# Later turns for the bias pieces, the right-hand sums and the first head loads; norm weights in the output weights; another root in the last step

## The chip, the cores and the metric

The kernel runs on one core of one Trainium2 chip. The metric is the device time of one execution in microseconds (us): the median of the runs. Before the change it is 1885.63 us (three runs, 1884.32 to 1886.45). Engines: PE is TensorE, DVE is VectorE, ACT is ScalarE, POOL is GpSimd, SP is SyncE, which here only issues DMAs.

## The reference

One encoder layer on x of 1024 tokens by 1024 features, float32. `rmsnorm(x, g)` is `x * rsqrt(mean(x*x) + 1e-6) * g`, `swiglu` is `(silu(x @ w_gate) * (x @ w_up)) @ w_down` with an inner width of 2816.

```python
h = swiglu(rmsnorm(x, ffn1_pre_g), ffn1_w_gate, ffn1_w_up, ffn1_w_down)
x = x + 0.5 * rmsnorm(h, ffn1_post_g)
q, k, v = heads(rmsnorm(x, mix_pre_g) @ w_qkv)        # 16 heads of 64
o_na  = neighbourhood_attention(q[:8], k[:8], v[:8], na_rel_bias)
o_dil = dilated_mixture_attention(q[8:], k[8:], v[8:], t5_rel_bias)
mixed = concat(rmsnorm(o_na, na_out_g), rmsnorm(o_dil, dil_out_g)) @ w_out
x = x + rmsnorm(mixed, mix_post_g)
h = swiglu(rmsnorm(x, ffn2_pre_g), ffn2_w_gate, ffn2_w_up, ffn2_w_down)
return x + 0.5 * rmsnorm(h, ffn2_post_g)
```

## The kernel before

Every float32 product is made of three matmuls: each operand is split into a rounded high part (ACT, a cast: `whi`, `hi`) and the rest (DVE, a subtraction: `wlo`, `lo`), and L268 to L270 multiply high by high, high by low and low by high. The large products also use a 2 by 2 block scheme with seven products in place of eight; its sums of weight blocks and of token blocks are made on DVE, and its partial results are combined on DVE and ACT as they leave PSUM. The names of the blocks are A11, A12, A22, S1 to S4 on the token side, T1 and T2 on the weight side.

The stages in order of time: the first norm and the first product rows (to about 80 us); the first feed-forward network, FFN1, with 22 blocks of gate and up weights (to about 460 us; a block in its full form takes about 19.3 us, the early ones 13.6 us), then the passes of its down product (`Passes`, tiles `pw`, `praw`); values and then q and k (`QKPairs`, about 700 to 910 us, the last of them 8 turns of 19.3 us); the dilated and the neighbourhood attention (about 910 to 1150 us); the output projection; the second feed-forward network (called FFN3 here, as in the code, about 1210 to 1882 us), whose last pass gives the output.

What sets the order of the work: PE's program is written by hand. Beside it stand queues that are drained as PE's program is written. `c.sums` and `c.steps` hold small closures, one of each run at every second slice of four of a product (`step`); `c.todo` holds one list of closures per block, a *turn* (`tick`, `plan`); `flush` runs all that is left at once. `one_a_turn` puts one step of a list into each turn from `first` on. `behind(f, engines)` ties what f records behind the last instruction recorded so far on these engines; without it a list scheduler of the language layer places the instruction on its engine by its own estimates. A queue of DMAs is in order of its engine: a DMA that waits on SP or POOL holds up those behind it.

The pieces that the change touches. *Right-hand sums* (`RightSums`, L314 to L337): for each of 11 pairs of down-weight blocks, two loads `tr` by SP (L324, L325, 1 MB), three subtractions in place on DVE (L333 to L335), and a store `ts<-tr` to DRAM by POOL (L336); the load of the next pair goes into the same single buffer, so it waits for the store to land. *Bias pieces* (`bias_steps`): tables made once, stores `nb`, `gab` and `stk` by POOL, spread over the turns of FFN1. *Head loads* (`load_head`): for a head of attention, `st<-qk` by POOL (L920, L921), `g<-gab`, and with a pair's first head `va` and `vb`, by SP (L983, L971, L975); `queued` runs it behind the turn's other work. *Operand* (`norm`, `tile`, `sums`, `put`): the norm of the tokens, its block sums (L240) and its transposes on PE (L176) with their two evictions (L177 on ACT, L178 on DVE). *Finish* (L723 on): square sums on ACT (L168), the gain (L730), the inverse root (L137 to L154), the residual (L747 or L762). *GroupNorm*: the norm of an attention group, L1234 for the scale, L1246 to L1251 for the transposes (`put`). *Weights* (L116, L117): the output weights, split in high and low.

At the end of a feed-forward network's blocks, `final` closes the memory of the weight loads and opens `praw`, the buffers of the down product's loads (L635, L638), in the same memory.

## Time and profile before

| | |
|---|---|
| median of the runs | 1885.63 us (1884.32 to 1886.45) |
| the profiled execution | 1884.22 us |
| its span, first to last instruction | 1882.5 us |
| busy: PE, DVE, ACT, POOL | 1840.9, 1318.3, 789.3, 324.2 us |
| mean granted TensorE clock | 0.995 |
| end of the last matmul, issue of the last output DMA | 1871.78, 1879.22 us |

The profiled execution is 1.72 us longer than its span; the times of the profile's rows count from the span's start. A row of the timeline gives start and duration in us, engine, line, operation, output and input tiles, and in brackets the idle time before it and what ended that. A row of the windows gives, for a stretch of the span, the busy time of each engine with its count of instructions, then the granted clock, the busy share of the DMA engines and what they moved. Busy times of PE count each matmul of 128 by 512 with 0.39 us, though the next starts 0.23 us later, so a PE that seems always busy is read better by its count of matmuls per stretch.

### The profile page before, as it was taken

The numbers are of one execution on the slowest core, as the hardware profiler recorded it, in microseconds if no ns is written. First come the engines' busy times: TensorE is split into PE (matmuls) and PEld (weight loads), VectorE is DVE, ScalarE is ACT, GpSimd is POOL, SyncE is SP. The second block draws the span as 40 slices with busy tenths as digits, with TensorE's granted clock in tenths as the row PEclk, the third lists the DMA queues.
The fourth block names the chain that finished last, engine by engine and source line by source line (L and its number), as shares of the span: only waits on it lengthen the run. The fifth ranks groups of instructions, "written<-read, shape, count | busy, mean of one in ns | idle before, by whom it ended". The sixth has DMA issues, their size and how long they took to land.

```text
span 1882.5 us, 25100 instructions
## 1 busy us (share of the span) xinstructions
PE 1840.9 (98%) x9048; PEld 1536.6 (82%) x9048; DVE 1318.3 (70%) x2212; ACT 789.3 (42%) x1283; POOL 324.2 (17%) x521
## 2 busy tenths in 40 slices
PE   7999999999999999999899999999999999999997
PEld 6878878888888878888799987878888788888886
DVE  7778787766565876577666766786878877654557
ACT  5422233334443546223477764453222333344342
POOL 2122122111000122222442300121111111110000
PEclk9999999999999999999999999999999999999999
DMA  7656676755986666658783732585456656486563
GB/s 273 222 195 208 188 266 227 242 186 201 345 290 205 246 211 225 210 178 263 236 283 113 253 129 79 178 306 176 157 190 223 241 203 233 178 296 205 190 225 134
DMA packets 164222, 405.15 MB, mean 215 GB/s; under 512 B 17857, under 2 KB 34465, under 8 KB 162050
## 3 DMA queue, kind: packets, MB, share of 16 engines
q1 hardware_dynamic: 114896, 228.82, 36.8%
q0 software_dynamic: 48336, 172.63, 25.7%
q10 hardware_dynamic: 866, 2.10, 0.3%
q8 instruction: 71, 1.16, 0.3%
q14 instruction: 53, 0.43, 0.1%
HBM read 277.47 MB, written 131.07 MB: 217 GB/s over the span
## 4 chain that ended last, share of the span: by engine, by line
PE 56%; issue 27%; DMA 7%; DVE 6%; POOL 3%; ACT 2%; SPq 0%; POOLq 0%; DVEq 0%; ACTq 0%
PE mmp L268 9%; PE mmp L270 9%; PE mmp L269 9%; PE accp L270 6%; PE accp L268 6%; PE accp L269 6%; PE po L1068 3%; DMA tr<-in_wd_dram 2%; PE ptp L956 2%; PE sp L1056 1%; DMA ts<-tr 1%; PE trp L176 1%; PE po L1189 1%; POOL g L591 1%; PE sp L1176 1%
## 5 line engine op out<-in xcount | busy, mean ns | idle before, releaser
L268 PE MATMUL mmp<-x,whi 128*128 128x512 f32 x1412 | 558.8, 396 | 10.0 <-DVE v L499 7.3
L270 PE MATMUL mmp<-x,wlo 128*128 128x512 f32 x1412 | 553.3, 392 | 3.0 <-DVE wlo L363 3.0
L269 PE MATMUL mmp<-x,whi 128*128 128x512 f32 x1412 | 552.6, 391 | 0.2 <-DVE x L1527 0.2
L268 PEld LDWEIGHTS mmp<-x,whi 128*128 128x128 f32 x1412 | 265.6, 188 | 70.6 <-issue 6.2
L270 PEld LDWEIGHTS mmp<-x,wlo 128*128 128x128 f32 x1412 | 265.5, 188 | 63.3 <-DVE wlo L363 4.4
L269 PEld LDWEIGHTS mmp<-x,whi 128*128 128x128 f32 x1412 | 265.8, 188 | 56.2 <-DVE x L1527 0.5
L640 DVE TENSOR_TENSOR pw<-praw,pw 128x1024 fp32r<-128x1024 f32 (+1 forms) x182 | 199.0, 1139 | 124.4 <-ACT pw L639 124.4
L362 ACT CAST whi<-wraw 128x1024 fp32r<-128x1024 f32 x126 | 132.0, 1050 | 330.8 <-PE mmp L269 258.0
L639 ACT CAST pw<-praw 128x1024 fp32r<-128x1024 f32 (+1 forms) x182 | 168.9, 983 | 203.6 <-PE accp L270 170.0
L268 PE MATMUL accp<-pw 128*128 128x512 f32 x600 | 234.4, 391 | 0.2 <-DVE hb L711 0.2
L270 PE MATMUL accp<-pw 128*128 128x512 f32 x600 | 233.5, 389 | 0.0
L269 PE MATMUL accp<-pw 128*128 128x512 f32 x600 | 233.4, 389 | 0.0
L363 DVE TENSOR_TENSOR wlo<-wraw,whi 128x1024 fp32r<-128x1024 f32 x126 | 153.8, 1223 | 19.9 <-ACT whi L362 19.9
L268 PEld LDWEIGHTS accp<-pw 128*128 128x128 f32 x600 | 112.6, 188 | 23.9 <-issue 0.6
L270 PEld LDWEIGHTS accp<-pw 128*128 128x128 f32 x600 | 112.6, 188 | 23.6
L269 PEld LDWEIGHTS accp<-pw 128*128 128x128 f32 x600 | 112.7, 188 | 23.0
L572 POOL DMA_DIRECT2D g<-sg x44 | 24.1, 548 | 424.7 <-DVE sg L565 253.4
L381 ACT COPY s<-mmp 128x512 f32<-128x512 f32 x52 | 30.5, 587 | 125.1 <-PE mmp L270 112.6
L528 DVE TENSOR_TENSOR c<-mmp,u 128x512 f32<-128x512 f32 x52 | 35.8, 688 | 53.6 <-PE mmp L270 53.6
L178 DVE TENSOR_TENSOR x<-trp,x 128x512 fp32r<-128x512 f32 x76 | 52.0, 688 | 24.9 <-ACT x L177 24.7
L453 DVE TENSOR_TENSOR wraw<-wraw 128x1024 f32<-128x1024 f32 x52 | 63.5, 1220 | 6.1 <-DMA wraw<-in_wqk_dram 5.4
L177 ACT CAST x<-trp 128x512 fp32r<-128x512 f32 x76 | 44.5, 587 | 42.6 <-PE trp L176 42.4
(281 smaller groups left out, 2788.6 us busy)
## 6 DMA issues: line engine op xcount, KB each, us to landing
praw<-g SPq DMA_DIRECT2D x70, 512.0 KB
wraw<-in_wg_dram SPq DMA_DIRECT2D x44, 512.0 KB
wraw<-in_wu_dram SPq DMA_DIRECT2D x44, 512.0 KB
tr<-in_wd_dram SPq DMA_DIRECT2D x44, 512.0 KB
g<-sg POOLq DMA_DIRECT2D x88, 256.0 KB, 4.3
ts<-tr POOLq DMA_DIRECT2D x22, 1024.0 KB, 5.0
praw<-ts SPq DMA_DIRECT2D x88, 256.0 KB
praw<-in_wd_dram SPq DMA_DIRECT2D x66, 256.0 KB
```

The source lines that it names most:

```text
L177: nc.scalar.copy(hi, ps)
L178: nc.vector.tensor_sub(lo, ps, hi.bitcast(F32))
L268: nc.tensor.matmul(out, ahi, bhi, start=start, stop=False, skip_group_check=go_on)
L269: nc.tensor.matmul(out, ahi, blo, start=False, stop=False, skip_group_check=go_on)
L270: nc.tensor.matmul(out, alo, bhi, start=False, stop=stop, skip_group_check=go_on)
L362: nc.scalar.copy(hi, raw)
L363: nc.vector.tensor_sub(lo, raw, hi.bitcast(F32))
L453: nc.vector.tensor_sub(r[:, 0:2], r[:, 1:3], r[:, 0:2])
L639: nc.scalar.copy(w[side][:, 0, :m], raw[:, :m])
L640: nc.vector.tensor_sub(w[side][:, 1, :m], raw[:, :m], w[side][:, 0, :m].bitcast(F32))
L956: c.nc.tensor.transpose(self.tps[:, j, :], self.probs[:, j * P:(j + 1) * P], c.ident)
L1068: nc.tensor.matmul(po[0][:, un * 2 + j], u.pt[:, 2 * j + t, :], rhs, start=t == 0, stop=t == 1)
```

## The change

In words, part by part:

1. *Output weights.* The gains `na_out_g` and `dil_out_g` are no longer multiplied into the attention's result. They are loaded as columns (`gcol`, two small loads at the start), and `Weights.prepare` multiplies each half of 512 columns by its gain: two ACTIVATEs with a scale and two scalar_tensor_tensors in place of one cast and one subtraction of 1024 columns. `GroupNorm.scale` becomes a tensor_scalar. Two broadcast loads (`gd`) go. In `GroupNorm.put` both high copies are recorded ahead of both low subtractions.
2. *Sums tied to their place.* `Operand.pinned` ties the norm's scale, its block sums and `Finish.rest`'s residual behind DVE's last recorded instruction. It is set at the start of FFN1 from turn 2 to turn 4, and for the second half of the values and q/k stage, whose `plan` also no longer flushes the queues first.
3. *Start of FFN1.* `two` and `fifth` normalise tokens 4 and 5 apart, the fifth two turns later; the transposes of tiles 6 and 7 come one turn earlier.
4. *Right-hand sums.* They begin at turn 9 in both networks (before: 7 in FFN1, 8 in FFN3).
5. *Bias pieces.* They begin at turn 8 in place of turn 0; two shifts a turn in turns 11 to 18, four rows a turn in turns 17 to 20.
6. *Head loads.* The first at turn 5 (before 4), the second at turn 6 behind `first_q` and `first_bias` (before at turn 5).
7. *Last step.* The gain's product goes to a tile of its own (`low`) for the first half, so that it needn't wait for the square sum; ACT's Sqrt and a reciprocal with one correction step take the place of the integer estimate with three steps.

```diff
 def prepare(self):
-    nc.scalar.copy(hi, raw)
-    nc.vector.tensor_sub(lo, raw, hi.bitcast(F32))
+    for j in range(2):
+        h, l, x = [y[:, j * T:(j + 1) * T] for y in (hi, lo, raw)]
+        g = gains[:, j:j + 1]
+        nc.scalar.activation(h, x, AF.Copy, scale=g)
+        nc.vector.scalar_tensor_tensor(l, x, g, h.bitcast(F32), op0=ALU.mult, op1=ALU.subtract)
...
+    def pin(self, f):
+        self.c.behind(f, *[DVE] * self.pinned)
-            self.c.sums.append(lambda i=i, n=n: self.tile(*n, r[:, i:i + 1]))
+            self.c.sums.append(lambda i=i, n=n: self.pin(lambda: self.tile(*n, r[:, i:i + 1])))
-            c.sums.append(lambda f=f, args=args: f(*args))
+            c.sums.append(lambda f=f, args=args: self.pin(lambda: f(*args)))
...
 def half(self, t, g, h):
-        self.c.nc.vector.tensor_mul(h, h, self.gain[:, g * T:(g + 1) * T])
+        to = h
+        if self.xt is not None and g == 0:
+            to = self.low[t] = self.c.xp.tile([P, T], F32, tag="low", name="low", bufs=2)
+        self.c.nc.vector.tensor_mul(to, h, self.gain[:, g * T:(g + 1) * T])
 def end(self, t, h):
-        nc.vector.tensor_scalar(q, self.ss[:, t, 1:2], 0.5 / D, 0.5 * EPS, op0=ALU.mult, op1=ALU.add)
-        r = rstd_of(c, self.ss[:, t, 0:1], D, q)
+        nc.vector.tensor_scalar(q, self.ss[:, t, 1:2], 1.0 / D, EPS, op0=ALU.mult, op1=ALU.add)
+        nc.scalar.activation(y, self.ss[:, t, 0:1], AF.Sqrt, bias=q, scale=1.0 / D)
+        nc.vector.tensor_scalar(k, q, -0.5, None, op0=ALU.mult)
+        nc.vector.scalar_tensor_tensor(v, self.ss[:, t, 0:1], -0.5 / D, k, op0=ALU.mult, op1=ALU.add)
+        nc.vector.reciprocal(y, y)
+        nc.vector.scalar_tensor_tensor(e, y, v, y, op0=ALU.mult, op1=ALU.mult)
+        nc.vector.scalar_tensor_tensor(y, e, 1.5, y, op0=ALU.add, op1=ALU.mult)
...
 class Finish: def rest(self, ts, h):
-            nc.vector.scalar_tensor_tensor(x, h(t), self.r[t], x, op0=ALU.mult, op1=ALU.add)
+            c.behind(lambda: nc.vector.scalar_tensor_tensor(x, h(t), self.r[t], x, op0=ALU.mult, op1=ALU.add),
+                     *[DVE] * (self.op is not None and self.op.pinned))
...
-    at = {0: [begin], 1: [lambda: table(0)], 2: [lambda: table(1)]}
+    at = {8: [begin], 9: [lambda: table(0)], 10: [lambda: table(1)]}
-        add(n, fill, 2 * n)
+        add(n + 8, fill, 2 * n)
-        add(n + 1, shifted, n)
+        add(n + 9, shifted, n)
-            add(2 * n + i + 4, shift, n, i)
-            add(n + 9, rows, 2 * n + i)
+            add(n + 11, shift, n, i)
+            add(17 + n // 2, rows, 2 * n + i)
...
 class GroupNorm:
-            self.c.nc.vector.scalar_tensor_tensor(o, o, self.r[:, i:i + 1], self.gain, op0=ALU.mult, op1=ALU.mult)
+            self.c.nc.vector.tensor_scalar(o, o, self.r[:, i:i + 1], None, op0=ALU.mult)
             nc.scalar.copy(hi, src)
+            parts.append((lo, src, hi))
+        for lo, src, hi in parts:
             nc.vector.tensor_sub(lo, src, hi.bitcast(F32))
...
-            one_a_turn(sums, NF, NF - 3 + (which == 3) - len(sums), tables(pool, bt))
+            one_a_turn(sums, NF, NF - 1 - len(sums), tables(pool, bt))
...
-  {0: [lambda: c.behind(F(4, 5), ACT), L(6, 7)], 3: [U(4)], 4: [F(6, 7), U(5)], 6: [U(6)], 7: [U(7)]},
+  {0: [lambda: c.behind(two, ACT), L(6, 7)], 2: [fifth], 3: [U(4)],
+   4: [lambda: setattr(op0, "pinned", False), F(6, 7), U(5)], 5: [U(6)], 6: [U(7)]},
...
-            plan(8, {1: [A(6, 7), U(5)], 3: [U(6)], 5: [U(7)]})
+            op.pinned = True
+            plan(8, {1: [A(6, 7), U(5)], 3: [U(6)], 5: [U(7)]}, False)
...
-            plan(8, {4: [lambda: queued(load_head)], 5: [lambda: queued(load_head)],
-                     6: [lambda: queued(first_q), lambda: queued(first_bias)]})
+            plan(8, {5: [lambda: queued(load_head)],
+                     6: [lambda: queued(first_q), lambda: queued(first_bias), lambda: queued(load_head)]})
```

How the change moves instructions, at three places. In the changed kernel the lines stand 8 further from the operand's code on and 20 further from the attention's code on.

SP, the last two turns of the q and k stage, before: the loads of head 0 (`g<-gab`, `va`, `vb`) stand ahead of the last block's `s<-s1d` and its two weight loads `wraw`.

```order
L355 DMA wraw<-in_wqk_dram 128x2x512
L356 DMA wraw<-in_wqk_dram 128x1024
L983 DMA g<-gab_68 128x384
L983 DMA g<-gab_69 128x384
L971 DMA va<-v_88 128x7x130
L971 DMA va<-v_88 128x2x130 x2
L975 DMA vb<-v_88 128x1x130 x8
L487 DMA s_7355<-s1d 128x512
L355 DMA wraw<-in_wqk_dram 128x2x512
L356 DMA wraw<-in_wqk_dram 128x1024
L983 DMA g<-gab_68 128x384
```

The same place in the changed kernel.

```order
L363 DMA wraw<-in_wqk_dram 128x2x512
L364 DMA wraw<-in_wqk_dram 128x1024
L495 DMA s_7355<-s1d 128x512
L363 DMA wraw<-in_wqk_dram 128x2x512
L364 DMA wraw<-in_wqk_dram 128x1024
L1003 DMA g<-gab_68 128x384
L1003 DMA g<-gab_69 128x384
L991 DMA va<-v_88 128x7x130
L991 DMA va<-v_88 128x2x130 x2
L995 DMA vb<-v_88 128x1x130 x8
```

The 13 loads of head 0 moved behind the last weight loads of the stage.

SP, the end of FFN1's blocks, before: `tr` are the loads of the right-hand sums, `praw` those of the down product.

```order
L324 DMA tr<-in_wd_dram 128x2x512
L325 DMA tr<-in_wd_dram 128x1024
L356 DMA wraw<-in_wu_dram 128x1024
L355 DMA wraw<-in_wg_dram 128x2x512
L356 DMA wraw<-in_wu_dram 128x1024
L635 DMA praw<-g_0_158 128x2x512
L638 DMA praw<-in_wd_dram 128x512 x2
```

The same place in the changed kernel.

```order
L332 DMA tr<-in_wd_dram 128x2x512
L333 DMA tr<-in_wd_dram 128x1024
L364 DMA wraw<-in_wu_dram 128x1024
L332 DMA tr<-in_wd_dram 128x2x512
L333 DMA tr<-in_wd_dram 128x1024
L643 DMA praw<-g_0_158 128x2x512
L646 DMA praw<-in_wd_dram 128x512 x2
```

The last loads of the sums moved to directly ahead of the down product's first loads.

DVE, the middle of the values and q/k stage (about 692 to 704 us), before: L762 is the residual of tokens 6 and 7, L178 the second eviction of the transposes, L363 the low parts of weights.

```order
L178 TENSOR_TENSOR x_5433<-trp,x_5432 128x4x128
L762 SCALAR_TENSOR_TENSOR x<-hb,y,x 128x1024
L178 TENSOR_TENSOR x_5425<-trp,x_5424 128x4x128
L762 SCALAR_TENSOR_TENSOR x<-hb,y,x 128x1024
L178 TENSOR_TENSOR x_5427<-trp,x_5426 128x4x128
L363 TENSOR_TENSOR pw<-graw,pw 128x1024
L178 TENSOR_TENSOR x_5429<-trp,x_5428 128x4x128
```

The same place in the changed kernel.

```order
L182 TENSOR_TENSOR x_5433<-trp,x_5432 128x4x128
L182 TENSOR_TENSOR x_5425<-trp,x_5424 128x4x128
L182 TENSOR_TENSOR x_5427<-trp,x_5426 128x4x128
L371 TENSOR_TENSOR pw<-graw,pw 128x1024
L182 TENSOR_TENSOR x_5429<-trp,x_5428 128x4x128
L182 TENSOR_TENSOR x_5431<-trp,x_5430 128x4x128
L371 TENSOR_TENSOR wlo<-graw,whi 128x1024
```

The two residuals left this run of evictions; they stand 16 and 18 rows further down, among the evictions of the next token tile.

More of the change, by code (lines that the diff above doesn't have):

```diff
@@ L185, in __init__ @@
     def __init__(self, c, gain, which):
-        self.c, self.gain, self.x, self.parts, self.wait, self.open = c, gain, {}, {}, deque(), 0
+        self.c, self.gain, self.x, self.parts, self.wait, self.open, self.pinned = c, gain, {}, {}, deque(), 0, False
         for b in (A11, A12):
@@ L1205, with __init__ @@
 class GroupNorm:
-    def __init__(self, c, og, b0, gain, strip, ot):
-        self.c, self.og, self.b0, self.gain, self.strip, self.ot = c, og, b0, gain, strip, ot
+    def __init__(self, c, og, b0, strip, ot):
+        self.c, self.og, self.b0, self.strip, self.ot = c, og, b0, strip, ot
     def squares(self, cols, part=0):
@@ L1246, in put @@
             nc.tensor.transpose(ps[:, j, :], o[:, j * P:(j + 1) * P], c.ident)
+        parts = []
         for hf in range(2):
@@ L1619, in begin, with two, scale, fifth @@
                 return s1
+            held = []
+            def two():
+                ts, xt, xns, ss = op0.squares([4, 5], [xs[4], xs[5]])
+                def scale():
+                    r = rstd_of(c, ss[:, :2], D)
+                    tiles = [lambda i=i: op0.tile(ts[i], xt[i], xns[i], r[:, i:i + 1]) for i in range(2)]
+                    c.sums.extend([tiles[0]] + [lambda: None] * 2)
+                    held.append(tiles[1])
+                c.sums.append(scale)
+            def fifth():
+                op0.pinned = True
+                c.sums.append(lambda: op0.pin(held.pop()))
             F = lambda *ts: lambda: op0.norm(ts, [xs[t] for t in ts])
@@ L1718, in layer @@
             s1.close()
-        dil, na = [[[a["wo"][g, i] for i in ii] for g in range(2)] for ii in ((0, 1), (2, 3))]
+        gcol = c.base.tile([P, 8], F32, name="gcol")
+        for i, n in enumerate(("dil_out_g", "na_out_g")):
+            nc.sync.dma_start(gcol[:, 4 * i:4 * i + 4], a[n].rearrange("o (k p) -> p (o k)", p=P))
+        dil, na = [[[(a["wo"][g, i], gcol[:, 2 * i:2 * i + 2]) for i in ii] for g in range(2)] for ii in ((0, 1), (2, 3))]
         c.w = Weights(c, dil[1] + dil[0] + na[1] + na[0] + dil[1] + na[1])
@@ L1728, in layer @@
             setattr(c, n, pool(n, b, st, space=PSUM))
-        gd = c.at.tile([P, D], F32, tag="gd", name="gd", bufs=1)
-        nc.sync.dma_start(gd[:, 0:512], a["na_out_g"].broadcast_to([P, 512]))
-        nc.sync.dma_start(gd[:, 512:D], a["dil_out_g"].broadcast_to([P, 512]))
         c.cmask = c.at.tile([P, 384], F32, tag="cmask", name="cmask", bufs=1)
@@ L1760, in attended @@
                           + weights + [lambda: None] + weights)
-        early = [GroupNorm(c, og[0], 4 * quad, gd[:, :512], True, None) for quad in range(2)]
+        early = [GroupNorm(c, og[0], 4 * quad, True, None) for quad in range(2)]
         def last(quad):
```

23 lines of the change are left out of this document (14 added, 9 removed).

## The prediction

> **What bounds the kernel now.** I read the page's busy times first, then what PE waited for, then windows of 20 us, and then the timelines of the engines where a window is short of matmuls.
>
> The page's first lines, and from the view of waits what PE waited for (us in all, times, longest):
>
> ```profile
> span 1882.5 us, 25100 instructions
> PE 1840.9 (98%) x9048; PEld 1536.6 (82%) x9048; DVE 1318.3 (70%) x2212; ACT 789.3 (42%) x1283; POOL 324.2 (17%) x521
> ...
> PE mmp L268 <- DVE v L499: 7.3, 3, 5.5
> ...
> PE trp L176 <- DVE x L178: 3.3, 6, 1.1
> PE mmp L270 <- DVE wlo L363: 3.0, 2, 1.7
> ...
> PE mmp L268 <- ACT u L381: 2.4, 2, 1.4
> PE trp L1246 <- DVE n L1251: 2.3, 5, 0.5
> PE trp L176 <- DVE xn L217: 1.1, 1, 1.1
> ```
>
> PE is the bound nearly everywhere, and the change leaves its matmuls as they are. So it can gain only what PE loses: these waits, the slower clock behind one of them, and the tail after the last matmul. DVE is 30% idle on average, yet most of the waits name it: it is late at certain places.
>
> What a wait costs is best read from the matmuls that a stretch lacks (x behind PE's busy time; the last three columns are the granted clock, the DMA share and GB/s):
>
> ```profile
> 220.00:240.00 20.00, 18.62 (x82) 14.91 (x81) 13.09 (x19) 5.26 (x7) 5.27 (x9) 1.00 0.65 198
> 240.00:260.00 20.00, 19.03 (x83) 15.29 (x82) 14.66 (x18) 7.21 (x11) 3.56 (x6) 1.00 0.72 253
> 400.00:420.00 20.00, 20.00 (x89) 16.37 (x88) 13.41 (x16) 6.60 (x9) 1.85 (x3) 1.00 0.40 134
> 880.00:900.00 20.00, 19.13 (x85) 15.51 (x83) 11.66 (x15) 6.14 (x9) 4.95 (x6) 1.00 0.80 272
> 900.00:910.00 10.00, 5.39 (x16) 4.34 (x17) 6.97 (x10) 2.85 (x5) 3.33 (x5) 0.66 0.91 315
> 1440.00:1460.00 20.00, 19.21 (x85) 15.51 (x84) 17.61 (x25) 5.52 (x7) 4.76 (x8) 1.00 0.76 275
> 1460.00:1480.00 20.00, 18.96 (x83) 15.25 (x82) 18.21 (x24) 6.38 (x9) 4.00 (x7) 1.00 0.77 262
> ```
>
> An undisturbed stretch has 89 in 20 us, 0.225 us each.
>
> **Head loads: −7.4.** SP's queue and then DVE, in the last turns of the q and k stage, and the first use of head 0 on PE:
>
> ```profile
> 870.11 0.79 SPq L983 DMA_DIRECT2D g<-gab  x2
> ...
> 875.64 6.50 SPq L975 DMA_DIRECT2D vb<-v  x8
> ...
> 897.09 1.23 DVE L453 TENSOR_TENSOR wraw<-wraw 128x1024 f32<-128x1024 f32 x1 [5.39 <-DMA wraw<-in_wqk_dram]
> ...
> 922.71 1.10 PE L1056 MATMUL semm<-st 128*128 128x256 f32 x8
> ```
>
> Head 0's loads hold SP from 870.11 to 882.14, 12 us; only then go the last block's weights. They land at 897.09, DVE has idled 5.39 us, v comes late, PE waits 5.5 us for it, and the clock of that window is 0.66. Its 16 matmuls are 28 to 29 short, 6.4 us; 880 to 900 lacks 4, 0.9 us: 7.3, with the first microseconds' slow clock in both I take 7.4. Behind the weights these 12 us of issue are off the path, as the stage's last matmuls need no load of SP after them. What is late next is the attention: if SP begins at about 886 it is done at about 898, and POOL's `st` for head 0 goes some 13 us later, while the first use comes at 915 instead of 923. Ends: 0 (the attention waits instead) and −7.6.
>
> **Right-hand sums in FFN1: −2.6.** DVE's waits for `tr`, the store's time to land (the median at the end of its row), and the eviction of v in two successive full turns:
>
> ```profile
> 231.74 1.23 DVE L333 TENSOR_TENSOR tr<-tr 128x1024 f32<-128x1024 f32 x1 [6.55 <-DMA tr<-in_wd_dram]
> ...
> 252.27 1.23 DVE L333 TENSOR_TENSOR tr<-tr 128x1024 f32<-128x1024 f32 x1 [5.11 <-DMA tr<-in_wd_dram]
> ...
> ts<-tr POOLq DMA_DIRECT2D x22, 1024.0 KB, 5.0
> ...
> 433.19 0.59 ACT L381 COPY v<-mmp 128x512 f32<-128x512 f32 x1 [1.33 <-PE mmp L270]
> ...
> 452.46 0.59 ACT L381 COPY v<-mmp 128x512 f32<-128x512 f32 x1 [0.43 <-PE mmp L270]
> ```
>
> Subtract, store (5.0 us), load into the same buffer: the chain took 20.5 us from one wait's end to the next, a full turn is 19.3 (433.19 to 452.46), an early turn shorter. Behind the waiting DVE stand c and u, and PE waits 2.4 us for u. The two windows lack 7 and 6 matmuls, 2.9 us; as DVE waited 11.7 us in all, some 4.4 of each wait cost PE nothing. In the new order the first pair is loaded in turn 9, and every subtraction lies in a full turn, in which the same chain is late by about 1 us, inside the 4.4. DVE's own work, 1.23 + 2 × 0.69 = 2.6 us a pair, meets 6.6 us of idle time in 20 (13.41 busy). The bias pieces now fall into the same turns; what hides them is the free share of the DMA engines, 0.28 to 0.60, and without it each microsecond beyond the 4.4 counts. Ends −0.5 and −2.9.
>
> **The same in FFN3: −2.0.** 1440 to 1480 lacks 4 + 6 matmuls, 2.2 us; DVE is 88 to 91% busy there, with a wait for `tr` besides:
>
> ```profile
> 1454.91 1.23 DVE L333 TENSOR_TENSOR tr<-tr 128x1024 f32<-128x1024 f32 x1 [2.07 <-DMA tr<-in_wd_dram]
> ```
>
> One turn later a pair's subtractions leave this place. Ends −0.9 and −2.2.
>
> **Values to q and k: −2.8.** The first of two residuals in DVE's order ahead of evictions (L178) and low weights (L363):
>
> ```profile
> 694.25 1.29 DVE L762 SCALAR_TENSOR_TENSOR x<-hb,y,x 128x1024 f32<-128x1024 f32 x1 [1.03 <-DMA x<-in_x_dram]
> ```
>
> With its idle time it takes 2.3 us, the second about as much. PE's longest wait for wlo, 1.7, and 1.2 of its 3.3 for x lie between 690 and 710, 2.9 in all. Put behind the next tile's evictions the residuals find their loads landed, and their norm still has a turn. Ends −1.5 (the evictions are late by themselves) and −3.3.
>
> **Start of FFN1: −1.2.** Two norms run back to back ahead of a low weight:
>
> ```profile
> 36.55 2.48 DVE L217 SCALAR_TENSOR_TENSOR xn<-x,y,gain 128x1024 f32<-128x1024 f32 x2
> ```
>
> PE waits the other 1.3 for wlo just behind them, and 1.1 for an x at 78 us, 2.4. One norm fewer takes 1.24 us from ahead of wlo; the transposes a turn earlier spread the second wait; but the fifth norm now falls among evictions that were on time, so I take half. Ends +0.5 and −2.4.
>
> **Output projection: −1.3.** Three successive rows of DVE between transposes:
>
> ```profile
> 1156.93 0.42 DVE L1251 TENSOR_TENSOR n<-trp,n 128x256 fp32r<-128x256 f32 x1 [0.44 <-ACT n L1250]
> 1157.27 0.74 DVE L1234 SCALAR_TENSOR_TENSOR og<-og,y,gd 128x512 f32<-128x512 f32 x1
> 1157.93 0.42 DVE L1251 TENSOR_TENSOR n<-trp,n 128x256 fp32r<-128x256 f32 x1
> ```
>
> Their period is 1.00 + 0.42 + 0.44 = 1.86 us, in which PE waits about 0.5, five times, so its own need is about 1.35. With both high copies first the idle 0.44 goes, and DVE needs some 1.42: under 0.1 is left of each wait, −1.8. That takes the tensor_scalar at the 0.74 of the operation it replaces, its nearest row by shape. Against it: a weight's low half becomes 2 × 0.74 for one 1.23 (the length of the 1024-column rows above), 0.25 more, and two of them stand ahead of the norm for which PE waits 1.1 (L217), +0.5. The scaled copies on ACT hide in its idle 58%. Ends 0 and −2.8.
>
> By the Trainium skill ("VectorE: DVE Perf Modes", section Mode 2×_2P) a float32 operation with a single tensor input in SBUF uses both read ports and gives two results a cycle. By that, as an estimate, the tensor_scalar would take about half of the 0.74, DVE would need less than PE, and this term would be −1.8. No row of this profile shows such an operation.
>
> **Last step: −3.4.** The last tiles on DVE, the last matmul, the last issue, and the group of two other table loads on ACT (busy, mean ns):
>
> ```profile
> 1869.87 0.69 DVE L730 TENSOR_TENSOR hb<-hb,gain 128x512 f32<-128x512 f32 x1 [0.85 <-ACT junk L168]
> ...
> 1872.39 1.42 DVE L747 SCALAR_TENSOR_TENSOR xl<-hb,y,xl 128x512 f32<-128x512 f32 x2
> 1873.72 0.68 DVE L714 TENSOR_TENSOR hb<-accp,hb 128x512 f32<-128x512 f32 x1
> ...
> 1871.39 0.39 PE L270 MATMUL accp<-pw 128*128 128x512 f32 x1
> ...
> 1879.22 0.34 ACTq L748 DMA_DIRECT2D out_dram<-xl  x1
> ...
> L551 ACT ACT_TABLE_LOAD x2 | 2.6, 1283 | 0.0
> ```
>
> DVE starts the last tile at 1873.72, 1.9 after PE's end at 1871.78; from there to the last issue are 5.5 us: 0.7 add, 0.85 idle, 0.7 gain, 1.8 for nine small operations, 1.4. After: the gain runs beside ACT's square; the root is a short operation on ACT (about 0.3 with its hand-over) and four on DVE of about 0.2 each, as the nine were. 0.7 + 0.9 + 0.3 + 0.8 + 1.4 = 4.1, or 4.0 with overlaps: 1.5 saved. DVE's work per tile falls to about 3.9, below PE's 21 × 0.2275 = 4.8, so the 1.9 go too. The table load, 1.28, falls on the first of four tiles and is made good by the third. Ends −2.5 and −4.0.
>
> **Last sums: +0.7.** The new risk. Before, `praw` is free at 436.03, right after the last low weight from the same memory; DVE then frees sg; later ACT casts `praw`, ahead of v:
>
> ```profile
> 436.03 0.38 SPq L635 DMA_DIRECT2D praw<-g  x1
> 438.63 0.69 DVE L565 TENSOR_TENSOR sg<-mmp,sg 128x512 f32<-128x512 f32 x1 [0.60 <-PE mmp L270]
> 447.45 1.05 ACT L639 CAST pw<-praw 128x1024 fp32r<-128x1024 f32 x1
> ```
>
> Now the sums' buffer, in that memory, is in use two turns longer. The last pair is subtracted behind sg, at 439.3 to 441.9; its store is issued at about 442.2 and lands at 447.2; `praw` is issued then, 11 us later than before, and if that load takes 4 us two casts end at 453.4 and v at 454.0. PE wants that bank when the next product of 12 matmuls ends, 2.7 after the 452.4 of v's own: 455.1. So about 1.1 us of slack, and the same in FFN3. Ends 0 and +5.
>
> The two gain columns at the start take two issues like the one above, 0.4 each, where SP is ahead: 0, at most +0.5.
>
> **Sum.** −7.4 − 2.6 − 2.0 − 2.8 − 1.2 − 1.3 − 3.4 + 0.7 = −20.0 us. The profiled execution took 1884.2, its span and 1.7 around it: 1864.2 after. The median of the runs lies 1.4 above that execution: **1865.6**, own range 1861 to 1871.
>
> **The rivals.** *DVE is late elsewhere* (22%). DVE's work hardly shrinks, and what is tied or later may meet other evictions. For it: every one of the middle waits names DVE or what DVE held up. Against: full turns leave a third of DVE free. Then half of the four middle terms and of the projection, 9.9 together, comes back, and the last sums cost 2.0: −20.0 + 5.0 + 1.3, 1871.9.
>
> *The stall only moves to the attention* (12%). Head 0's loads now end close to their first use, where the DMA share is 0.91. For it: that share. Against: some 15 us from the end of issue to use. Without that term, 1873.0.
>
> *More than the forecast* (12%): the projection at −1.8 (0.5 more), the four middle terms and the last step at their far ends (2.8 more), no loss at `praw` (0.7): 1861.6. For it: DVE idles 30%, and each of these waits is short. Against: all of them would have to go together.
>
> *The last sums hold up the down product, slower* (3%). The place is `praw` in both networks. If store, load and cast there take 10 us more than the slack, v comes at about 465, PE idles 10 us and loses 1.9 more to a slow clock, as it did around 900: 2 × 11.9 against −20.7, 1888.7. It decides from some 9 us beyond the slack in each network on. For it: a chain of store and load has taken over a turn. Against: the DMA share in these turns is 0.40.
>
> *It doesn't do what it says* (3%): the list scheduler brings the old order back; about 1882.
>
> **Chances.** The forecast has 48%. The range for 8 in 10 takes in most of the first three rivals: 1859 to 1875. A measurement here tells 0.2%, 3.8 us, from nothing. Faster 0.94, same 0.03, slower 0.03.
>
> **What would show it.** 900 to 910 with 44 matmuls at full clock, and no wait of L453 for `wraw`; no wait of PE for u in FFN1; DVE's last L722 less than 0.3 us after the last matmul, and about 4 us from there to the last issue; no idle time of ACT for `praw` beyond 2 us ahead of v. I am wrong if PE waits for `va`, `st` or their copies at the start of the attention, or if the turns 20 and 21 of a network lack over 10 matmuls.

## The result

The changed kernel takes 1868.41 us (median of four runs, 1866.51 to 1870.32), the one before, beside it, 1886.04 (four, 1884.32 to 1886.99). The ratio is 0.9908, 95% interval 0.989 to 0.9925: 17.6 us faster. The forecast was 1865.6 in a range of 1859 to 1875. The profiled execution took 1868.1 around a span of 1866.1, 16.4 less than the span before.

The page of the changed kernel, and its view of what PE waited for (us in all, times, longest), answer to the first rows of the prediction:

```profile
span 1866.1 us, 25121 instructions
PE 1838.7 (99%) x9048; PEld 1534.3 (82%) x9048; DVE 1318.9 (71%) x2208; ACT 795.5 (43%) x1300; POOL 324.8 (17%) x521
```

```profile
PE trp L180 <- DVE xn L225: 2.3, 2, 1.7
PE mmp L276 <- DVE v L507: 1.8, 1, 1.8
...
PE trp L180 <- DVE s L248: 1.5, 1, 1.5
PE mmp L276 <- ACT s L389: 1.2, 1, 1.2
PE trp L180 <- DVE x L182: 1.1, 4, 0.4
...
PE accp L276 <- DVE hb L719: 0.7, 1, 0.7
```

DVE has as much work as before, 1319 us. Gone are the waits for wlo and u, most of those for v and x, and those for n in the output projection. Two of those that remain are new, for the sums s behind a norm and for the copy s of ACT; that for hb grew from 0.2 to 0.7, that for xn from 1.1 to 2.3. The windows in which matmuls were lacking (busy us and instructions of PE, PEld, DVE, ACT and POOL, then clock, DMA share, GB/s):

```profile
215.00:235.00 20.00, 20.00 (x86) 15.36 (x85) 13.63 (x20) 5.94 (x8) 6.20 (x11) 1.00 0.43 131
...
895.00:905.00 10.00, 10.00 (x46) 8.29 (x45) 5.18 (x7) 3.25 (x5) 1.58 (x3) 1.00 0.69 231
905.00:915.00 10.00, 8.21 (x40) 6.63 (x40) 7.50 (x9) 1.47 (x4) 8.18 (x9) 1.00 0.77 248
1435.00:1455.00 20.00, 20.00 (x89) 16.43 (x88) 18.10 (x24) 5.53 (x7) 3.60 (x7) 1.00 0.83 291
```

PE is busy throughout in all but one. The stretch that had 16 matmuls at a clock of 0.66 (900 to 910 before, about 895 to 905 now) has 46 at full clock. The window behind it, 905 to 915, is short of PE time by 1.8 us, and POOL is busy in it for 8.2 of 10 us.

Both kernels have the same 9048 matmul rows on PE, with the same count ahead of each stage, so the start of the k-th can be compared in the two traces. The table is worked out in this way, stage by stage (negative: the changed kernel is quicker; the forecast's +0.7 for the last sums is halved between the two networks):

| stage | matmuls | forecast, us | measured, us |
|---|---|---|---|
| up to 21 us | to 50 | 0 | +0.4 |
| start of FFN1 | 50 to 340 | −1.2 | −0.3 |
| right-hand sums in FFN1 | 340 to 1300 | −2.6 | −2.7 |
| rest of FFN1, with its last sums | 1300 to 2900 | +0.35 | +0.7 |
| values to q and k | 2900 to 3700 | −2.8 | −1.7 |
| head loads | 3700 to 4250 | −7.4 | −4.9 |
| attention | 4250 to 5750 | 0 | −0.7 |
| output projection | 5750 to 6150 | −1.3 | −3.3 |
| start of FFN3 | 6150 to 7000 | 0 | +0.6 |
| right-hand sums in FFN3 | 7000 to 7500 | −2.0 | −2.2 |
| rest of FFN3, with its last sums | 7500 to 9040 | +0.35 | +1.2 |
| last step, behind the last matmul | | −3.4 | −3.5 |
| sum | | −20.0 | −16.4 |

### The profile page after: what moved, and what is told of

Same layout as the page of the kernel before. It is cut to its first block, busy times and chain, and to the rows that moved or that the text cites. A ratio compares the mean times of both kernels' runs of the same rounds, so it can differ in the third digit from the quotient of the medians.

```text
span 1866.1 us, 25121 instructions
## 1 busy us (share of the span) xinstructions
PE 1838.7 (99%) x9048; PEld 1534.3 (82%) x9048; DVE 1318.9 (71%) x2208; ACT 795.5 (43%) x1300; POOL 324.8 (17%) x521
## 4 chain that ended last, share of the span: by engine, by line
PE 81%; issue 10%; DVE 4%; DMA 2%; ACT 2%; POOL 0%; DVEq 0%; ACTq 0%; SPq 0%; POOLq 0%
PE mmp L276 17%; PE mmp L278 17%; PE mmp L277 17%; PE accp L276 7%; PE accp L278 7%; PE accp L277 7%; PE po L1088 3%; PE ptp L976 2%; PE po L1209 1%; PE trp L180 1%; PE sp L1076 1%; PE sp L1196 1%; DMA xn<-xn 0%; DMA sgd<-sg 0%; DVE x L182 0%
## 5 line engine op out<-in xcount | busy, mean ns | idle before, releaser
L371 DVE TENSOR_TENSOR wlo<-wraw,whi 128x1024 fp32r<-128x1024 f32 x126 | 154.4, 1227 | 20.2 <-ACT whi L370 20.1
```

Of the source, the lines that this page charges most:

```text
L371: nc.vector.tensor_sub(lo, raw, hi.bitcast(F32))
```

## The experiments

Each is the changed kernel with one edit (two, far apart, or three where that is said), profiled once; only the changed kernel and the last run were timed four times. They are compared with it by the same table, matmul by matmul. Over most of the kernel two executions agree there to 0.1 us. At a few places they differ without any edit: by up to 3.9 us at the start of FFN1 (told there), up to 2.0 at the norm behind the output projection (about 1192 us), up to 2.1 at the first casts of `praw` (about 456), and about 1 in the attention, in FFN3's first and last stretches and at a few other points. So a whole time says little here, and an edit's effect is read at its own place.

### The first head loads back in their old turns

```diff
-plan(8, {5: [lambda: queued(load_head)],
-         6: [lambda: queued(first_q), lambda: queued(first_bias), lambda: queued(load_head)]})
+plan(8, {4: [lambda: queued(load_head)], 5: [lambda: queued(load_head)],
+         6: [lambda: queued(first_q), lambda: queued(first_bias)]})
```

> The changed kernel with the first two head loads back in turns 4 and 5. Theory: SP's queue is the cause, head 0's 13 loads stand ahead of the last block's weights again; L461 waits for wraw by about 5 us, PE loses about 7.3 us near 897, and the new wait for v (L507, 1.8 us, at 911) goes, since POOL's copies for head 0 fall later: PE is about 5.4 us later from the attention on, the span about 1871.5. Rival: the gain of 7.3 came from the removed gain loads and the DMA time they took, not from the queue; then L461 waits under 1 us and the span stays within 1.5 us of 1866.1.

Measured 1874.98 us. In this stage it loses 5.9 us: DVE waits for the weights again, PE for v, and the clock falls. A window and DVE's row:

```profile
900.00:910.00 10.00, 6.42 (x19) 5.14 (x20) 5.95 (x8) 3.12 (x5) 2.52 (x3) 0.66 0.87 283
```

```profile
896.08 1.22 DVE L461 TENSOR_TENSOR wraw<-wraw 128x1024 f32<-128x1024 f32 x1 [5.90 <-DMA wraw<-in_wqk_dram]
```

The place of the head loads is the cause of the stall. But the stall costs 8.4 at its place; 2.1 come back behind it, as the late wait for v at 910 is not there in this kernel, and 0.5 near 933. The next two runs ask where that wait comes from.

How the place makes the weights late is not separated. In the kernel before, their buffer was free at 882.4 (the end of the last row that read it, of L363) and they were issued at 884.54, so the queue of issues held them for only some 2 us of the 12 that the prediction named. They were there for DVE 12.5 us after that issue, against at most 9.2 in the changed kernel (issued at 878.77, used without a wait at 887.94). So most of the delay is time to land, just behind head 0's loads.

### The copies on POOL for the first head

In the changed kernel POOL works beside DVE from 904 on:

```profile
904.47 0.88 POOL L947 COPY g<-g 128x384 f32<-128x384 f32 x1 [8.42 <-DMA g<-gab]
...
905.87 2.42 POOL L947 CAST q<-st 128x1024 fp32r<-128x1024 f32 x1
908.23 1.32 POOL L947 COPY g<-g 128x384 f32<-128x384 f32 x1
...
918.05 2.14 POOL L947 CAST q<-st 128x1024 fp32r<-128x1024 f32 x1
```

and DVE's rows, in the same stretch:

```profile
904.51 1.92 DVE L371 TENSOR_TENSOR wlo<-wraw,whi 128x1024 fp32r<-128x1024 f32 x1 [0.17 <-ACT whi L370]
906.35 2.48 DVE L920 TENSOR_TENSOR qk<-c,qk 128x512 fp32r<-128x512 f32 x1
908.75 1.34 DVE L920 TENSOR_TENSOR qk<-qk 128x512 fp32r<-128x512 f32 x1
910.02 0.68 DVE L507 TENSOR_TENSOR v<-mmp,u 128x512 f32<-128x512 f32 x1
...
918.19 0.41 DVE L965 CUSTOM_DVE_ANT_1 s<-sp,g 128x256 f32<-128x256 f32 x1
```

A row of L371 takes 1.23 us elsewhere, one of L920 0.68 in the two turns before. Here they take 1.92, 2.48 and 1.34, together 3.2 more, and v, for which PE waits, stands behind them. Their ends tell more: 906.43, 908.83 and 910.09 lie 1.08, 0.54 and 0.54 us behind the ends of the POOL rows beside them (905.35, 908.29, 909.55), which is each row's usual duration less 0.15. So DVE does next to nothing until POOL is done. The row at 918.19, which reads one operand from PSUM, runs beside the next cast at its usual length.

On this the Trainium skill says ("SBUF — State Buffer", section "SBUF: two separate sides") that a GpSimd operation that reads SBUF and a VectorE operation with two inputs in SBUF share a pair of ports under an exclusive lock: the one that comes first has it for its whole instruction. The ends of the rows agree with that. The trace of the kernel before has such a row too: at 898.35 one of L454, 0.69 us elsewhere, took 1.24 and ended 0.55 behind POOL's copy of g (897.57 to 899.04). The prediction did not weigh it: its step "head loads" asked what SP and the attention would find, not what POOL's copies would find on DVE.

First run: the cast of q and the second copy of g one turn later; the copy at 904 stays.

```diff
-6: [lambda: queued(first_q), lambda: queued(first_bias), lambda: queued(load_head)]
+6: [lambda: queued(load_head)],
+7: [lambda: queued(first_q), lambda: queued(first_bias)]
```

> The changed kernel with POOL's two copies for the first head (q and its bias, L947) one turn later, in turn 7; nothing else moves ahead of the attention. Theory: the copies that POOL makes in SBUF at 904 to 909.5 stretch DVE's rows at the same time (L371 to 1.92, L920 to 2.48 and 1.34 where 1.23 and 0.69 are usual), so v is late and PE waits 1.8 us; with the copies later these rows have their usual length and PE has no wait for L507: 1.9 us earlier at the attention's start, less whatever the attention then waits for q. Rival: the DMA traffic or the late data stretch them; then L371 and L920 near 905 stay above 1.3 us together with the wait of 1.8.

Measured 1871.75 us. The rows of L920 take 0.68 again and PE's wait for v at 910 is gone, 2.1 us. The row of L371, still beside the copy that stayed (904.60 to 905.48), takes 1.60 and ends 1.08 behind it. But DVE's first rows of the attention need g, which POOL now copies after the cast of q:

```profile
918.12 0.42 DVE L965 CUSTOM_DVE_ANT_1 ses<-semm,g 128x256 f32<-128x256 f32 x1 [3.78 <-POOL g L947]
```

PE waits 3.04 for them, and the stage is 3.1 us slower than in the changed kernel. Second run: only the cast goes, the copies of g stay.

```diff
-6: [lambda: queued(first_q), lambda: queued(first_bias), lambda: queued(load_head)]
+6: [lambda: queued(first_bias), lambda: queued(load_head)], 7: [lambda: queued(first_q)]
```

> Only the first head's cast of q goes from turn 6 to turn 7 of the q and k stage; the two copies of g stay in turn 6. Theory, that POOL's copies stretch DVE's rows beside them and so make v late at 910: the 2.42 us cast no longer lies beside L920, whose rows take 0.7 to 1.3, PE's wait for v at 910.85 (1.95 us more than a matmul's pitch) falls to under 0.5, and the cast, which would run from about 915 to 917.3, is done before the first product with q at about 919: 1.5 us less up to the attention. Rival, that DVE's rows are late by their own order: the wait for v stays over 1.5. Rival, that the cast at 915 holds up the attention as the move of all three did: a wait of over 1.5 us between 915 and 922.

Measured 1869.10 us, with 2.5 us lost at the start of FFN1, far from the edit. At its own place it gains 2.1 us; PE waits nowhere between 907 and 917:

```profile
907.00:917.00 10.00, 10.00 (x49) 8.43 (x48) 6.92 (x13) 3.53 (x6) 6.16 (x8) 1.00 0.76 263
```

```profile
908.73 1.36 DVE L920 TENSOR_TENSOR qk<-c,qk 128x512 fp32r<-128x512 f32 x1
```

This row is still stretched, beside the second copy of g (908.23 to 909.54), and again it ends 0.55 behind it. The cause of the new wait at 910 is shown: take the cast away from DVE's rows and the wait goes. Over the stage only 1.1 us are left, where I had expected 1.5, as 1.0 is lost again near 930 in the same way: POOL's next cast now begins with a row of L920 that took 0.69 in the changed kernel, and a copy of g follows it.

```profile
928.25 2.07 POOL L947 CAST q<-st 128x1024 fp32r<-128x1024 f32 x1 [5.03 <-DMA st<-qk]
```

```profile
928.31 2.57 DVE L920 TENSOR_TENSOR qk<-qk 128x512 fp32r<-128x512 f32 x1 [0.77 <-ACT qk L919]
```

### High and low in turn again

```diff
-    parts.append((lo, src, hi))
-for lo, src, hi in parts:
     nc.vector.tensor_sub(lo, src, hi.bitcast(F32))
```

> The changed kernel with the copies and subtractions of the output's transposes (high, low, high, low) in their order of before. Theory: the order removes an idle time of 0.44 us on DVE per tile; with it back DVE's period is 0.42 + 0.44 + 0.45 + 0.42 less overlaps, about 1.6 us against PE's 1.35 or less, so PE loses about 0.25 us in each of five to six tiles, 1.4 us. Rival: the short tensor_scalar (0.48) alone takes DVE below PE; then PE's waits for the transposes stay under 0.3 us in all.

Measured 1868.48 us. In the projection's transposes it is 1.9 us slower than the changed kernel (1.4 expected). PE's rows there, a transpose of each tile, first of this run and then of the changed kernel:

```profile
1147.37 0.63 PE L1266 MATMUL trp<-ident,og 128*128 128x128 f32 x4 [0.26 <-DVE n L1271]
1148.96 0.63 PE L1266 MATMUL trp<-ident,og 128*128 128x128 f32 x4 [0.26 <-DVE n L1271]
```

```profile
1148.72 0.60 PE L1266 MATMUL trp<-ident,og 128*128 128x128 f32 x4
1149.86 0.60 PE L1266 MATMUL trp<-ident,og 128*128 128x128 f32 x4
```

The period of a tile is 1.59 here, 1.14 in the changed kernel and was 1.86 before. So the order of the two copies is worth 0.45 a tile, and the shorter operation on DVE 0.27.

### The flush and the free placement back, between values and q and k

```diff
-op.pinned = True
-plan(8, {1: [A(6, 7), U(5)], 3: [U(6)], 5: [U(7)]}, False)
+plan(8, {1: [A(6, 7), U(5)], 3: [U(6)], 5: [U(7)]})
```

> The changed kernel with the second half of the values and q/k stage as before (flushed, nothing tied). Theory: tying the residuals and the norm of tokens 6 and 7 gained 3.9 us near 700 and cost 2.3 us near 720, where PE now waits 0.6 for xn and 1.5 for s; so both come back, PE waits for wlo by 1.7 and for x by 1.2 again and not at 720, 1.6 us more in all. Rival: the waits at 720 are not from the tie (the norm of two tiles back to back is late anyway); then they stay and PE is 3.9 us later.

Measured 1874.11 us. Up to about 714 us it is 5.3 us slower than the changed kernel: PE waits 1.7 for wlo, 0.5 for pw and 1.7 for an x again. Then 2.3 come back: in the changed kernel DVE makes two norms in one go, ahead of the sums of the first, and PE waits for both.

```profile
718.59 2.48 DVE L225 SCALAR_TENSOR_TENSOR xn<-x,y,gain 128x1024 f32<-128x1024 f32 x2
...
722.72 0.68 DVE L248 TENSOR_TENSOR s<-xn 128x512 f32<-128x512 f32 x1
```

The move does remove the waits that it was costed on, and more of them than I had counted; it makes new ones behind them, of 0.7 and 1.7 us. If the two norms are their cause, it should help to make them one at a time:

```diff
-for i, n in enumerate(zip(ts, xs, xns)):
-    self.c.sums.append(lambda i=i, n=n: self.pin(lambda: self.tile(*n, r[:, i:i + 1])))
+tiles = [lambda i=i, n=n: self.pin(lambda: self.tile(*n, r[:, i:i + 1])) for i, n in enumerate(zip(ts, xs, xns))]
+if self.pinned and len(tiles) == 2:
+    self.c.sums.append(lambda: [tiles[0](), self.c.sums.append(tiles[1])])
+else:
+    self.c.sums.extend(tiles)
...
-c.sums.extend([lambda: None] * 2 + [lambda t=t, x=x: add(t, x) for t, x in zip(ts, xs)])
+c.sums.extend([lambda: None] * (1 if self.op is not None and self.op.pinned else 2)
+              + [lambda t=t, x=x: add(t, x) for t, x in zip(ts, xs)])
```

> Between values and q and k, the last two token tiles are normed one at a time, the second behind the first one's four sums, and the residuals ahead of them come one step earlier. Theory, that the two new waits of PE (0.73 us for xn at 720 and 1.69 for the sums behind it at 723.5) come from the two norms standing back to back, 2.48 us, and from the residuals' step: both waits fall to under 0.4, about 1.8 us less at the end of the q and k transposes. Rival, that the loads behind the residuals and the sums are not there a step earlier: DVE waits for a load there and a wait of over 1 us stays.

Measured 1868.38 us. At its place it gains 1.4 us:

```profile
719.57 1.29 DVE L228 SCALAR_TENSOR_TENSOR xn<-x,y,gain 128x1024 f32<-128x1024 f32 x1
720.89 0.69 DVE L251 TENSOR_TENSOR s<-xn 128x512 f32<-128x512 f32 x1
...
725.64 1.27 DVE L228 SCALAR_TENSOR_TENSOR xn<-x,y,gain 128x1024 f32<-128x1024 f32 x1
```

The sums begin behind the first norm, and the second norm stands behind the last of them. The waits for the norm and for the sums are gone, some 2.5 us, so the two norms in one go, with the step of the residuals that moved too, are their cause. A new wait of 0.8 us for an x costs about 1 of that, so the gain falls short of the 1.8 expected.

### Sums and bias pieces in FFN1, each put back alone

```diff
-one_a_turn(sums, NF, NF - 1 - len(sums), tables(pool, bt))
+one_a_turn(sums, NF, NF - 3 + (which == 3) - len(sums), tables(pool, bt))
```

> The right-hand sums of both networks start in their old turns again (first pair in turn 7 of FFN1, 8 of FFN3); the bias pieces and the rest stay as changed. Theory, that the stores and reloads of these pairs met turns too short or too full for them: PE waits for u come back in FFN1 (two, about 2.2 us together against the changed kernel) and DVE's wait for tr in FFN3 (about 2.4 us), in all +4.6 us, less about 0.2 if the sums at the networks' ends free their buffer earlier. Rival, that moving the bias pieces out of the early turns made FFN1's gain: FFN1 loses under 0.5 us here, FFN3 its 2.4.

Measured 1869.23 us. In FFN3 1.5 us are lost, in a wait of PE for v as before the change. In FFN1 it is 1.0, and not in a wait for u:

```profile
PE tabp L838 <- DMA oh<-in_onehot_dram: 0.9, 1, 0.9
```

DVE's waits for `tr` in the two turns where they were 6.55 and 5.11 us before the change:

```profile
226.88 1.23 DVE L341 TENSOR_TENSOR tr<-tr 128x1024 f32<-128x1024 f32 x1 [4.91 <-DMA tr<-in_wd_dram]
...
243.09 1.22 DVE L341 TENSOR_TENSOR tr<-tr 128x1024 f32<-128x1024 f32 x1 [0.22 <-issue]
```

And the other half of the pair:

```diff
-at = {8: [begin], 9: [lambda: table(0)], 10: [lambda: table(1)]}
+at = {0: [begin], 1: [lambda: table(0)], 2: [lambda: table(1)]}
...
-    add(n + 8, fill, 2 * n)
+    add(n, fill, 2 * n)
...
-    add(n + 9, shifted, n)
+    add(n + 1, shifted, n)
...
-        add(n + 11, shift, n, i)
-        add(17 + n // 2, rows, 2 * n + i)
+        add(2 * n + i + 4, shift, n, i)
+        add(n + 9, rows, 2 * n + i)
```

> Only the bias pieces go back to turn 0 and after in FFN1; the sums stay in their new turns. Theory, that the turn of the sums decides and the pieces are small beside it: the matmuls of FFN1 end within 0.5 us of the changed kernel's. Rival, that the pieces held up DVE in the early turns: PE loses 1.5 to 2.5 us between 150 and 260 us.

Measured 1867.31 us, 0.6 us below the changed kernel's profile at the last matmul. The bias tables' own matmuls on PE, 1.4 us, move from one stretch of FFN1 to another; over matmuls 340 to 1300 the difference is 0.0, inside the 0.5 expected. PE waits for u in neither run. So neither theory of the first run holds: neither the turn of the sums nor that of the pieces alone made the stall, it takes both in the early turns (about 222 to 262 us), and moving either one away is enough in FFN1. The time that the pairs' loads took fits that. Their issues on SP before the change, and with the sums alone in these turns:

```profile
222.31 0.55 SPq L324 DMA_DIRECT2D tr<-in_wd_dram  x1
...
240.19 0.55 SPq L324 DMA_DIRECT2D tr<-in_wd_dram  x1
```

```profile
218.36 0.55 SPq L332 DMA_DIRECT2D tr<-in_wd_dram  x1
...
235.11 0.54 SPq L332 DMA_DIRECT2D tr<-in_wd_dram  x1
```

Up to DVE's subtraction it was 9.4 and 12.1 us before the change (231.74 and 252.27, quoted in the prediction); with the sums alone it is 8.5 and at most 8.0. In the changed kernel both share turns again, but full ones: there DVE waits for `tr` in eight pairs, 1.2 to 3.9 us each, and PE for nothing.

```profile
363.85 1.23 DVE L341 TENSOR_TENSOR tr<-tr 128x1024 f32<-128x1024 f32 x1 [3.93 <-DMA tr<-in_wd_dram]
```

With the pieces back in the early turns and the sums in the full ones, none of these waits is over 0.5 us. In FFN3, where there are no pieces, the turn of the sums counts by itself.

### The old order at the start of FFN1

```diff
-{0: [lambda: c.behind(two, ACT), L(6, 7)], 2: [fifth], 3: [U(4)],
- 4: [lambda: setattr(op0, "pinned", False), F(6, 7), U(5)], 5: [U(6)], 6: [U(7)]},
+{0: [lambda: c.behind(F(4, 5), ACT), L(6, 7)], 3: [U(4)], 4: [F(6, 7), U(5)], 6: [U(6)], 7: [U(7)]},
```

> The first eight turns of FFN1 get their old norms, transposes and sums, not tied to their place. Theory, that the ties removed two waits of PE (1.5 us for a low weight behind the two norms, 1.2 us for x at 78 us) but a wait for the store of the gate's first product, whose landing varies by 2 us between executions, now shows in their place: the two waits come back, the wait of the copy s behind that store hides behind the first, and 340 matmuls in, the time is within 0.5 us of the changed kernel's own, or of the slowest of its runs. Rival, that the ties are worth the 1.2 us forecast and the wait for the store is chance: 1 to 1.5 us later than the changed kernel's profile at the same matmul.

Measured 1867.71 us. PE's waits for wlo (1.2) and for x (the longest 1.1) are back, and from matmul 50 to 340 it takes 1.9 us more than the profile of the changed kernel. But that profile is one of the better executions. ACT's copy s, for which PE waits in the new order, must itself wait for a store, here in the changed kernel and in the run that changes only the last step's root:

```profile
43.79 0.59 ACT L389 COPY s<-mmp 128x512 f32<-128x512 f32 x1 [1.89 <-DMA sgd<-s]
```

```profile
45.56 0.59 ACT L389 COPY s<-mmp 128x512 f32<-128x512 f32 x1 [3.78 <-DMA sgd<-s]
```

Over the ten profiled executions that have the new start unaltered (the changed kernel's own among them), the stretch takes 0.3 less to 3.6 us more than in the changed kernel's profile, 1.3 more on average; the two with the old one (this run and the kernel before) 0.3 and 1.9 more. So the tied norms bring nothing here that these executions can show. The store, issued at 36.2 to 37.4 us on POOL's queue in the ten, landed between 42.8 and 45.7.

### Two more edits: the store on SP's queue, and later transposes

```diff
-nc.gpsimd.dma_start(d, sg)
+(nc.gpsimd if s1 is None else nc.sync).dma_start(d, sg)
...
-3: [A(2, 3)], 4: [U(0)], 5: [U(1)],
+3: [A(2, 3)], 5: [U(0)], 6: [U(1)],
```

> Two edits far from each other. (1) In the output projection, the transposes of the first two normed tiles are asked for one turn later, behind 6 matmuls more: PE's wait for xn at 1191.67 (1.72 us) falls to 0.2 to 0.4, 1.4 us less; rival, the wait moves on to the low weights, which end at 1189.5, and nothing is gained. (2) At the start of FFN1 the stores of the first two gate products go out on SP's queue in place of POOL's, where they stood behind a wait of 4.84 us for another store: issued at about 36 in place of 37.07, so landed about 1 us earlier, and PE's wait for the copy s (1.2 us in the changed kernel's profile, 0.9 to 3.6 over all executions with this start) falls by 1 us; rival, the landing is set by the traffic of that time and not by the issue: landing after 43.5 all the same.

Measured 1869.49 us. ACT's copy s starts at 42.16, where it started at 43.79, and PE's wait for it falls to 0.3 us; but 1.2 us for an x stand behind it. The stretch takes as long as in the changed kernel's profile (0.1 more), so 1.2 less than the average of the ten; but some of the ten are as quick, so one run doesn't show the gain. The later transposes gain nothing: the wait of 1.7 us for xn at 1192 goes, and one of 0.3 for an x at 1200 and one of 1.5 for xn at 1209 come. From matmul 6050 to 6300 this run takes 0.3 us more than the changed kernel's profile, and the runs without this edit 0.1 less to 2.0 more.

### The root of the last step back on DVE

```diff
-nc.vector.tensor_scalar(q, self.ss[:, t, 1:2], 1.0 / D, EPS, op0=ALU.mult, op1=ALU.add)
-nc.scalar.activation(y, self.ss[:, t, 0:1], AF.Sqrt, bias=q, scale=1.0 / D)
...
+nc.vector.tensor_scalar(q, self.ss[:, t, 1:2], 0.5 / D, 0.5 * EPS, op0=ALU.mult, op1=ALU.add)
+y = rstd_of(c, self.ss[:, t, 0:1], D, q)
```

> The last step's root is computed by DVE's chain of small operations again; the gain's own buffer beside the square on ACT stays. Theory, that the root saved about 0.8 of the tail directly and kept DVE level with PE besides: DVE's work per tile grows by about 0.8 to 1.0 us to about 4.7, just below the 4.8 that PE takes for a tile, so the last tile starts at most 0.5 later and the tail after the last matmul is 0.8 to 1.4 us longer, 8.0 to 8.6 in place of 7.18. Rival, that the gain beside the square gives nearly all of it: under 0.3 us longer. Rival, that the root alone gives it: the tail is back at 10.2 to 10.7 us.

Measured 1871.16 us, with 3.6 us lost at the start of FFN1 (the store above). The tail behind the last matmul is 1.1 us longer than in the changed kernel, 8.3 in place of 7.2. The last tile in this run and in the changed kernel:

```profile
1861.00 0.68 DVE L722 TENSOR_TENSOR hb<-accp,hb 128x512 f32<-128x512 f32 x1
...
1865.12 0.74 DVE L759 SCALAR_TENSOR_TENSOR xl<-hb,y,xl 128x512 f32<-128x512 f32 x1
```

```profile
1858.94 0.69 DVE L722 TENSOR_TENSOR hb<-accp,hb 128x512 f32<-128x512 f32 x1 [0.89 <-PE accp L278]
...
1860.74 0.16 DVE L760 RECIPROCAL y<-y 128x1 f32<-128x1 f32 x1 [0.17 <-ACT y L757]
...
1862.06 0.74 DVE L765 SCALAR_TENSOR_TENSOR xl<-hb,y,xl 128x512 f32<-128x512 f32 x1
```

From the first to the last of these rows it is 4.1 us with the old root, 3.1 with the new. DVE, at 4.8 us a tile, then keeps just level with PE, with no idle time ahead of L722 (0.89 in the changed kernel). So of the 3.5 us saved, the root gives 1.1 and the gain's own buffer, beside ACT's square, with the tile's start that it makes earlier, 2.4.

### Three of the edits together

The cast of q in turn 7, the norms one at a time, and the first stores on SP's queue.

> The changed kernel with three of the edits tried alone: the first head's cast of q one turn later, the last two norms between values and q and k one at a time, and the first stores of the gate products on SP's queue. Theory, that these mend three different waits which do not touch: 1.1 us from the cast and 1.9 from the norms, as each took alone, and 0 to 1.5 from the stores, where a wait for the transposes' x takes over most of it: 3 to 4.5 us below the changed kernel's median of 1868.4, so 1864 to 1865.5, about 1.1% below the kernel before. Rival, that the time won in one place is lost in the next, as when the transposes were asked for later: within 1.5 us of 1868.4.

Measured 1866.79 us (four runs, 1864.49 to 1867.72); against the kernel before the ratio is 0.9897, interval 0.988 to 0.9913. That overlaps with the changed kernel's interval, so it is not shown to be faster, and the 1864 to 1865.5 expected was missed. At their places the edits do what they did alone, or a little better (in the profiled execution −1.4 and −2.1 us at the norms and the cast, and the better case at the store). But this execution loses 3.6 us between matmuls 1300 and 2350, in turns that no edit touches: PE waits for u, and at 456 us for v, since ACT stands before it in a cast whose load has not landed:

```profile
454.83 1.05 ACT L650 CAST pw<-praw 128x1024 fp32r<-128x1024 f32 x1 [2.50 <-DMA praw<-in_wd_dram]
455.78 0.58 ACT L392 COPY v<-mmp 128x512 f32<-128x512 f32 x1
```

In the changed kernel the same casts did not wait and v came in time:

```profile
449.09 1.98 ACT L647 CAST pw<-praw 128x1024 fp32r<-128x1024 f32 x2
450.98 0.57 ACT L389 COPY v<-mmp 128x512 f32<-128x512 f32 x1
```

This is the place of the slack of about 1 us that the prediction gave to the last sums. In three of the runs above the same cast waited too: 2.25 us in the one with the flush back, which lost 1.1 us there, and about 1.6 in those with the old start of FFN1 and with high and low in turn, which lost 0.5 each. Why the load is later in some executions is not settled.

## Why the prediction was right, and where not

The direction, the size and the range held; the likeliest time was 2.8 us too low. That it was no further off is partly luck: the head loads gave 2.5 us less than forecast, and the output projection 2.0 more, through two mis-sized numbers. Of the rivals, "DVE is late elsewhere" came true in part: new waits for DVE appeared at two of the places that were costed, and they cost 4.5 us together (2.1 at v, 0.7 and 1.7 at the norms).

- *Head loads (−7.4, measured −4.9).* The stall is gone, and so is the slow clock, and at their place that gained the 7.4 forecast. The step that failed is "what is late next is the attention": next was v at 910, behind rows of DVE that POOL's copies held up, which took 2.1 back; another 0.5 went near 933. The far end given for the term, 0, had the wrong mechanism but covered it. The 12 us on SP's queue, too, explain the lateness of the weights only in part (first run above).
- *Right-hand sums in FFN1 (−2.6, measured −2.7).* The size is right, the reason only in part. I put the gain down to full turns in which the chain of store and load is late by about 1 us, inside the 4.4 that PE doesn't feel. Full turns do hide it, but it is late by up to 3.9 there. And the two runs show that this move was not the only cure: the early turns stalled only with the bias pieces in them too, and either move is enough.
- *The same in FFN3 (−2.0, measured −2.2).* Right; put back, 1.5 of it returns.
- *Values to q and k (−2.8, measured −1.7).* The waits named went. The words "their norm still has a turn" failed: two norms of 1.24 us, one behind the other, made PE wait 0.7 and 1.7 us.
- *Start of FFN1 (−1.2, measured −0.3; over all executions no gain is shown).* The waits for wlo and x were removed, but ahead of them the wait for a store decides, which I had not looked for: the copy s waits for it in the kernel before too.
- *Output projection (−1.3, measured −3.3, beyond the far end of −2.8).* Two numbers of the sum were mis-sized. PE's own need is 1.14 us a tile, not 1.35: I had subtracted the idle time of the row, 0.53, from the period, but idle time is counted from the end of the matmul before, whose row is 0.39 long, while its successor could start after 0.23. A wait costs about 0.2 us more than its row says; 1.86 to 1.14 is 0.72 a tile. And the operation that I took at 0.74 takes 0.48:

```profile
1147.30 0.48 DVE L1254 TENSOR_SCALAR og<-og,y 128x512 f32<-128x512 f32 x1
1147.75 0.76 DVE L1274 TENSOR_TENSOR n<-trp,n 128x256 fp32r<-128x256 f32 x2
1148.43 0.48 DVE L1254 TENSOR_SCALAR og<-og,y 128x512 f32<-128x512 f32 x1
```

  DVE needs 1.13 us a tile (1147.30 to 1148.43), just below PE. The Trainium skill's rule, cited in the prediction ("VectorE: DVE Perf Modes", section Mode 2×_2P), pointed the right way: DVE then needs less than PE. The half that I worked out from it would have been 0.37; the row is 0.48, so the measurement lies between the half and the 0.74 of the sum. The loss of 0.5 for the weights' halves was taken at its right size: PE's wait for xn at 1192 grew from 1.1 to 1.7 (to 2.0 or 2.1 in three other executions).
- *Last step (−3.4, measured −3.5).* Right in its parts too: the last tile starts 0.04 us after PE's end, and the last issue comes 3.9 us behind that.
- *Last sums (+0.7).* In the profile nothing is lost at `praw`, so the +0.7 of the table has another cause (next point). But the chain is as close as was said: four of the runs above lost 0.5 to 2.1 us there.
- *Not foreseen:* −0.7 in the attention, +0.6 at the start of FFN3 and +0.5 in a wait for hb ahead of the last tiles, all three no larger than executions differ there without an edit; and about 0.7 in each network's full turns: from 265 to 460 us a matmul follows the one before after 230.4 ns on average, before the change after 229.3, and no row of a view shows a wait there. The runs with the sums and with the pieces back have 230.4 too, so neither move is its cause. That is left open.

## What to carry to other kernels

When a stall is removed, look at every engine that shares something with the engine waited for, not only at the next wait in line: here a copy on an otherwise idle engine took back 2.1 of 7.4 us. Cost a removed wait by the distance between the starts of the work it holds up, not by the idle time of its row. And when two moves of one change meet in the same turns, undo each alone before believing the reason for the gain.
